# The 64-token block inverse of a chunked recurrence on TensorE: one factor held in the other chunk's half, and products issued by turns

## The chip, the cores and the metric

One core of a Trainium2 chip runs the whole program once. The metric is device microseconds of one execution. A core has TensorE (PE, with its weight loads shown as PEld), VectorE (DVE), ScalarE (ACT), GpSimd (POOL) and the queue engine SyncE (SP), 16 DMA engines, SBUF, and eight PSUM banks.

## The reference

Two transformer blocks of two layers each, 256 tokens, model width 1024, all in fp32. Everything that is changed here belongs to one branch of the second block: a linear recurrence of 8 heads of width 64 with a decaying state, which runs in both layers.

```python
def step(state, inp):
    r_t, w_t, k_t, v_t, a_t, b_t = inp
    sa = jnp.einsum('bhvk,bhk->bhv', state, a_t)
    state = (state * w_t[:, :, None, :] + sa[..., None] * b_t[:, :, None, :]
             + v_t[..., None] * k_t[:, :, None, :])
    return state, jnp.einsum('bhvk,bhk->bhv', state, r_t)
...
y = rwkv7_scan(rh, decay, kh, vh, -kk, kk * ah)
```

Beside it, in the same layer, stand a sparse attention branch (with a top-k search over 256 keys), two sigmoid gates and the output projections; then a memory attention, and a feed-forward or a mixture of experts.

## The kernel before

The 256 tokens are cut into four chunks of 64, and the recurrence inside a chunk is written as matrix products: `AB` holds the products of A with B of all pairs of a chunk's tokens (and those of R with B), `AK` the same with K. The unit lower triangular matrix that belongs to `AB` is inverted block by block: `Tm` and its transpose `TT` start at blocks of 2 and are doubled in five levels, `lv` = 2, 4, 8, 16, 32. A level is X = mask(AB^T Tm) (L1567, then DVE L1570), TT += X^T TT (L1575, DVE L1582) and, but for the last level, Tm += TT^T X (L1580, DVE L1581). With `TT` follow the products by V (L1598), U (L1609), the transform WT of A (L1619), and then the serial part over the four chunks: U += WT S (L1636, DVE L1638), the next state from K, V, B and U (L1642, L1644), and the outputs (L1667, L1674).

All these are products of 64 by 64 matrices. A product that reads partitions 0 to 63 uses the upper half of the array's rows, one that reads 64 to 127 the lower; the partitions of its PSUM output choose the half of the columns. So a product sits in one of four corners of the array. `half(par)` is the half that holds the even or odd chunk of a pair `t`, `half(hf)` that of a head in a pair of heads `i`, `ch(c)` the columns of chunk c. `bank()` hands out PSUM banks; the recurrence has four of the eight.

One pass of `rwkv_group` handles 4 of the 8 heads, so it runs twice a layer and four times in all (called groups here). The two generators of a layer are advanced by turns. Each `yield n` reports n units of work, and `mixer2` calls so many steps of the dense work of the layer (the columns, gates and projections, L645 and L667, of some 12 matmuls a step, and the sparse attention, L1741 to L1796) for them:

```python
for work in self.rwkv(l, vfirst):
    due[0] += self.RATES[len(ready)] * work
    due[1] += self.RATES[2] * work * len(ready)
```

What is left of the dense work then runs behind. A scheduler of the build sets the final order on each engine. Weights are split into two parts of lower precision by ACT L473 and DVE L474; the top-k search is DVE L1751 to L1757.

Of the kernel before, what the change touches and what calls it, by code (L numbers as in the profile page):

```python
# [14 lines left out]
ALU = mybir.AluOpType  # L15
# [346 lines left out]
class Builder:  # L362
# [967 lines left out]
    def rwkv(self, l, vfirst):  # L1330
# [37 lines left out]
        A.copy(sel, self.ident[0:8, 0:8, None].to_broadcast([8, 8, 64]))  # L1368
# [83 lines left out]
    def rwkv_group(self, l, g, GD, tail, R, K, Vv, WA, ld, w2a, rnT, a0h, kah, nkah, ys, bonus):  # L1452
# [42 lines left out]
        V.scalar_tensor_tensor(f(Bt), f(Bt), 0.5, f(E3), op0=ALU.mult, op1=ALU.mult)  # L1495
        AR = self.t([2, 2, 256], "AR")
        V.scalar_tensor_tensor(AR[:, :, 0], kkn, -1.0, E1, op0=ALU.mult, op1=ALU.mult)
        V.tensor_tensor(AR[:, :, 1], R[:, J], E2, op=ALU.mult)
# [31 lines left out]
        def inside(src, nm):  # L1530

            r = {}
            for hf in range(2):
                b = self.bank().rearrange("p (t j k c) -> p t j k c", t=2, j=2, k=2)
                d = r[hf] = self.t([2, 2, 2, 64], nm)
                for t in range(2):
                    for i in range(2):
                        for par in range(2):
                            c = ch(2 * t + par)
                            PE.matmul(b[half(par), t, i], lhsT=src[half(hf), i, c], rhs=AR[half(hf), i, :, c], start=True, stop=True)  # L1540
                fl = lambda z: z.rearrange("p t j k c -> p (t j) (k c)")
                V.tensor_tensor(fl(d), fl(b), self.cc["kmask"][:, None, :].to_broadcast([P, 4, P]), op=ALU.mult)
            return r
# [5 lines left out]
        for hf in range(2):  # L1549
            b = self.bank().rearrange("p (u c) -> p u c", u=8)  # L1550
            for t in range(2):
                for i in range(2):
                    for par in range(2):
                        c = ch(2 * t + par)
                        PE.matmul(b[half(par), 2 * t + i], lhsT=AR[half(hf), i, 0, c], rhs=Bt[half(hf), i, c], start=True, stop=True)
            V.tensor_tensor(Tm[:, hf], b[:, 0:4], m8("lv1", 4), op=ALU.mult)
            V.tensor_tensor(TT[:, hf], AB[hf].rearrange("p t j k c -> p (t j) k c")[:, :, 0], m8("lv1T", 4), op=ALU.mult)
# [5 lines left out]
        for lv in (2, 4, 8, 16, 32):  # L1563
            b = self.bank().rearrange("p (u c) -> p u c", u=8)
            for u, (hf, t, i) in enumerate(un):
                for par in range(2):
                    PE.matmul(b[half(par), u], lhsT=AB[hf][half(par), t, i, 0], rhs=Tm[half(par), hf, 2 * t + i],  # L1567
                              start=True, stop=True)
# [24 lines left out]
        for k in range(2):  # L1593
            b = self.bank().rearrange("p (t c) -> p t c", t=2)
            for t in range(2):
# [4 lines left out]
            if k == 0:  # L1600
                self.evac(akv, b)
            else:
                A.copy(yg, b.rearrange("p t (h c) -> p t h c", h=4))
            yield 1
        b = self.bank().rearrange("p (t c) -> p t c", t=2)
        for t in range(2):
            for h in range(4):
                for par in range(2):
                    PE.matmul(b[half(par), t, hc(h)], lhsT=TT[half(par), h % 2, 2 * t + h // 2], rhs=akv[half(par), t, hc(h)],  # L1609
                              start=True, stop=True)  # L1610
# [3 lines left out]
        WT = self.t([2, 4, 64], "WT")  # L1614
        for par in range(2):
            b = self.bank().rearrange("p (u c) -> p u c", u=8)
            for t in range(2):
                for h in range(4):
                    PE.matmul(b[half(h % 2), 2 * t + h // 2], lhsT=At[half(par), t, hc(h)], rhs=TT[half(par), h % 2, 2 * t + h // 2],  # L1619
                              start=True, stop=True)  # L1620
            self.evac(WT[:, par], b[:, 0:4])
# [8 lines left out]
        for c in range(4):  # L1630
# [39 lines left out]
            for hf in range(2):  # L1670
                b = self.bank().rearrange("p (u c) -> p u c", u=8)
                for cc in range(max(1, 2 * t), 2 * t + 2):
                    for i in range(2):
                        PE.matmul(b[half(cc % 2), i], lhsT=Rt[half(hf), i, ch(cc)], rhs=Sb[cc][half(hf), i], start=True, stop=True)  # L1674
# [612 lines left out]
```

## Time and profile before

| what | value |
|---|---|
| median of 3 runs | 2567.77 us (2567.64 to 2573.2) |
| the profiled execution's own time | 2573.59 us |
| its span | 2571.8 us, 40556 instructions |
| PE busy | 2498.0 us, 97% |
| PEld busy | 2129.9 us, 83% |
| DVE busy | 1936.2 us, 75% |
| ACT busy | 1319.6 us, 51% |
| chain that ended last | PE 88%, DVE 7%, ACT 2%, DMA 2% |

The profile is of one execution. A busy engine is one that has an instruction under way; matmuls overlap, so the busy time of PE says less than how far the starts of its bursts lie apart. Each fp32 matmul of the program appears in the trace as two matmul records, so counts there are twice those of the program's order. PEclk is the granted share of TensorE's clock, 1.00 being 2.4 GHz and 0.50 being 1.2 GHz.

### The profile page before, as it was taken

The numbers are of one execution on the slowest core, as the hardware profiler recorded it, in microseconds if no ns is written. First come the engines' busy times: TensorE is split into PE (matmuls) and PEld (weight loads), VectorE is DVE, ScalarE is ACT, GpSimd is POOL, SyncE is SP. The second block draws the span as 40 slices with busy tenths as digits, with TensorE's granted clock in tenths as the row PEclk, the third lists the DMA queues.
The fourth block names the chain that finished last, engine by engine and source line by source line (L and its number), as shares of the span: only waits on it lengthen the run. The fifth ranks groups of instructions, "written<-read, shape, count | busy, mean of one in ns | idle before, by whom it ended". The sixth has DMA issues, their size and how long they took to land.

```text
span 2571.8 us, 40556 instructions
## 1 busy us (share of the span) xinstructions
PE 2498.0 (97%) x16346; PEld 2129.9 (83%) x16346; DVE 1936.2 (75%) x3247; ACT 1319.6 (51%) x1967; POOL 75.6 (3%) x77
## 2 busy tenths in 40 slices
PE   8999999999999999999999998999999988999998
PEld 7887788888888788888888877888988877888887
DVE  6779767777777676777686478778685577999998
ACT  4445444444444444544544445445434345788786
POOL 0001000000000000000010000000100000000000
PEclk9999999999999999999999989999999998999999
DMA  6445344554564353555413244555211336998995
GB/s 258 180 176 197 130 165 151 193 200 173 184 226 169 142 203 154 184 193 190 177 34 117 97 164 148 184 200 195 104 63 60 140 121 240 355 344 337 346 337 199
DMA packets 77716, 477.74 MB, mean 186 GB/s; under 512 B 9936, under 2 KB 14928, under 8 KB 26832
## 3 DMA queue, kind: packets, MB, share of 16 engines
q1 hardware_dynamic: 77520, 475.06, 50.2%
q8 instruction: 130, 2.13, 0.3%
q14 instruction: 66, 0.54, 0.1%
HBM read 473.98 MB, written 1.05 MB: 185 GB/s over the span
## 4 chain that ended last, share of the span: by engine, by line
PE 88%; DVE 7%; ACT 2%; DMA 2%; issue 1%; SPq 0%; POOL 0%; DVEq 0%; ACTq 0%
PE bank L581 18%; PE bank L903 11%; PE bank L2076 9%; PE bank L582 9%; PE bank L645 8%; PE bank L717 6%; PE bank L2036 5%; PE bank L667 3%; PE bank L685 3%; DVE area L474 3%; PE bank L701 1%; PE bank L741 1%; PE bank L995 1%; DMA area<-w 1%; PE bank L1567 1%
## 5 line engine op out<-in xcount | busy, mean ns | idle before, releaser
L473 ACT ACTIVATE area<-area 128x1024 fp32r<-128x1024 f32 (+4 forms) x981 | 944.5, 975 | 714.8 <-PE bank L581 249.4
L474 DVE TENSOR_TENSOR area<-area,area 128x1024 fp32r<-128x1024 f32 (+4 forms) x981 | 1070.4, 1115 | 263.2 <-ACT area L473 258.5
L581 PE MATMUL bank<-area 128*128 128x512 f32 x2208 | 790.5, 400 | 4.0 <-DVE area L474 3.0
L582 PE MATMUL bank<-area 128*128 128x256 f32 x2208 | 619.1, 282 | 0.4 <-DVE area L474 0.4
L581 PEld LDWEIGHTS bank<-area 128*128 128x128 f32 x2208 | 415.2, 188 | 111.4 <-issue 6.8
L582 PEld LDWEIGHTS bank<-area 128*128 128x128 f32 x2208 | 417.8, 189 | 8.0 <-DVE area L474 2.1
L903 PE MATMUL bank<-area 128*128 128x512 f32 x1320 | 323.5, 396 | 4.0 <-ACT area L473 2.4
L903 PEld LDWEIGHTS bank<-area 128*128 128x128 f32 x1320 | 244.3, 190 | 59.2 <-DVE area L474 4.3
L586 DVE TENSOR_REDUCE area<-bank 128x256 f32<-128x512 f32 x276 | 190.2, 689 | 89.2 <-PE bank L582 88.5
L2076 PE MATMUL bank<-area 128*128 128x512 f32 (+1 forms) x1152 | 257.0, 373 | 0.0
L645 PE MATMUL bank<-area 128*128 128x256 f32 x1824 | 243.8, 290 | 1.4 <-ACT area L473 1.4
L645 PEld LDWEIGHTS bank<-area 128*128 128x128 f32 x1824 | 228.4, 195 | 7.2 <-ACT area L473 2.6
L2076 PEld LDWEIGHTS bank<-area 128*128 128x128 f32 x1152 | 209.6, 188 | 29.9
L717 PE MATMUL bank<-area 128*128 128x512 f32 x672 | 160.6, 395 | 2.4 <-DVE area L748 1.6
L717 PEld LDWEIGHTS bank<-area 128*128 128x128 f32 x672 | 125.1, 189 | 28.7 <-DVE area L748 2.0
L473 ACT ACTIVATE area<-bank 128x512 fp32r<-128x512 f32 (+2 forms) x154 | 82.9, 565 | 93.8 <-PE bank L741 34.5
L2036 PE MATMUL bank<-area 128*128 128x512 f32 x528 | 131.0, 392 | 0.0
L474 DVE TENSOR_TENSOR area<-bank,area 128x512 fp32r<-128x512 f32 (+2 forms) x154 | 97.0, 645 | 39.4 <-ACT area L473 39.3
L749 POOL TENSOR_TENSOR area<-area 128x1 f32<-128x1 f32 (+3 forms) x68 | 68.8, 1012 | 1902.2 <-DVE area L748 1780.6
L2036 PEld LDWEIGHTS bank<-area 128*128 128x128 f32 x528 | 97.6, 188 | 18.9
L950 ACT COPY area<-bank 128x512 f32<-128x512 f32 (+1 forms) x103 | 50.7, 498 | 99.0 <-PE bank L995 39.7
L685 PE MATMUL bank<-area 128*128 128x512 f32 x384 | 96.5, 401 | 3.7 <-ACT area L473 2.0
(281 smaller groups left out, 2231.1 us busy)
## 6 DMA issues: line engine op xcount, KB each, us to landing
area<-w SPq DMA_DIRECT2D x396, 1024.0 KB, 4.9
area<-w SPq DMA_DIRECT2D x32, 768.0 KB, 6.0
area<-rows SPq DMA_DIRECT2D x24, 512.0 KB, 6.7
area<-w SPq DMA_DIRECT2D x10, 512.0 KB, 5.5
area<-mem SPq DMA_DIRECT2D x8, 512.0 KB, 6.5
area<-cbias SPq DMA_DIRECT2D x8, 512.0 KB, 6.1
area<-w SPq DMA_DIRECT2D x2, 800.0 KB, 6.4
area<-x SPq DMA_DIRECT2D x2, 512.0 KB, 5.4
```

The lines of the kernel that those rows point to most:

```text
L473: return (self.A.activation(hi, src, AF.Copy), self.V.tensor_tensor(lo, src, hi.bitcast(F32), op=ALU.subtract))
L474: self.V.tensor_tensor(lo, src, hi.bitcast(F32), op=ALU.subtract))
L581: self.PE.matmul(bank[:, : 2 * n].rearrange("p (u c) -> p u c", u=2), lhsT=a[0], rhs=b.both, start=start, stop=False)
L582: self.PE.matmul(bank[:, n : 2 * n], lhsT=a[1], rhs=b[0], start=False, stop=stop)
L586: return self.V.tensor_reduce(out, ps.rearrange("p (u c) -> p c u", u=2), axis=AX.X, op=ALU.add)
L645: self.PE.matmul(bank[:, g * 256 : g * 256 + 256], lhsT=a, rhs=b, start=j == 0, stop=j == 3 * kt - 1)
L667: self.PE.matmul(bank[:, t, :n], lhsT=a[:, t, k], rhs=b, start=k == 0 and j == 0, stop=k == kt - 1 and j == 2)
L685: self.PE.matmul(bank[:, :n], lhsT=a[:, t, k], rhs=b, start=k == 0 and j == 0, stop=k == kt - 1 and j == 2)
L717: self.PE.matmul(acc[t][h], lhsT=a[:, t, k], rhs=b, start=k == 0 and j == 0, stop=k == kt - 1 and j == 2)
L903: self.PE.matmul(acc[t][h], lhsT=a[:, t * P : (t + 1) * P], rhs=b, start=m == 0 and j == 0, stop=m == n - 1 and j == 2)
L2036: self.PE.matmul(acc[hh], lhsT=x[:, k, :], rhs=y, start=c0 == 0 and k == 0 and j == 0, stop=c0 + n == E_DIM and k == n // P - 1 and j == 2)
L2076: PE.matmul(bk, lhsT=x[:, k, i * P : (i + 1) * P], rhs=y, start=k == 0 and j == 0, stop=k == 7 and j == 2)
```

## The change

`AR`, which holds A and R, is written with the two chunks of a pair exchanged, by four products instead of two, and its sign moves into the selector matrix (-1 in place of 1) and into B. So a matrix that is the left factor of one chunk sits in the half of the other one, and `Tm` and `X` come to lie in another half than `AB` and `TT`. The first `TT` is now made by products of its own (L1562) instead of being taken out of `AB`. In the levels, the two products that end a level are issued by turns, two corners for one (L1584) and two for the other (L1586); `inside` (L1541) goes through both heads of a pair by turns, the products by V (L1605) through both right-hand sides, and those of WT (L1626) through both chunks. Two banks are held at a time where one was before. A level below 32 yields 2 units where it yielded 3, and the products by V 1 where they yielded 2.

```diff
-        V.scalar_tensor_tensor(f(Bt), f(Bt), 0.5, f(E3), op0=ALU.mult, op1=ALU.mult)
+        V.scalar_tensor_tensor(f(Bt), f(Bt), -0.5, f(E3), op0=ALU.mult, op1=ALU.mult)
...
-        V.scalar_tensor_tensor(AR[:, :, 0], kkn, -1.0, E1, op0=ALU.mult, op1=ALU.mult)
-        V.tensor_tensor(AR[:, :, 1], R[:, J], E2, op=ALU.mult)
+        v4 = lambda z, a: z.rearrange("p j (t a c) -> p j t a c", t=2, a=2)[:, :, :, a]
+        for a in range(2):
+            V.tensor_tensor(v4(AR[:, :, 0], 1 - a), v4(kkn, a), v4(E1, a), op=ALU.mult)
+            V.tensor_tensor(v4(AR[:, :, 1], 1 - a), v4(R[:, J], a), v4(E2, a), op=ALU.mult)
...
-            for hf in range(2):
-                b = self.bank().rearrange("p (t j k c) -> p t j k c", t=2, j=2, k=2)
-                d = r[hf] = self.t([2, 2, 2, 64], nm)
-                for t in range(2):
-                    for i in range(2):
+            r, b = {}, [self.bank().rearrange("p (t j k c) -> p t j k c", t=2, j=2, k=2) for _ in range(2)]
+            for t in range(2):
+                for i in range(2):
+                    for hf in range(2):
                         for par in range(2):
                             c = ch(2 * t + par)
-                            PE.matmul(b[half(par), t, i], lhsT=src[half(hf), i, c], rhs=AR[half(hf), i, :, c], start=True, stop=True)
+                            PE.matmul(b[hf][half(par), t, i], lhsT=src[half(hf), i, c], rhs=AR[half(hf), i, :, ch(2 * t + 1 - par)], start=True, stop=True)
...
+                for hf in range(2):
+                    for par in range(2):
+                        c = ch(2 * t + par)
+                        PE.matmul(b[hf][half(1 - par), 1, 2 * t + i], lhsT=Bt[half(hf), i, c], rhs=AR[half(hf), i, 0, ch(2 * t + 1 - par)], start=True, stop=True)
...
-            V.tensor_tensor(TT[:, hf], AB[hf].rearrange("p t j k c -> p (t j) k c")[:, :, 0], m8("lv1T", 4), op=ALU.mult)
+            V.tensor_tensor(TT[:, hf], b[hf][:, 1], m8("lv1T", 4), op=ALU.mult)
...
-                    PE.matmul(b[half(par), u], lhsT=AB[hf][half(par), t, i, 0], rhs=Tm[half(par), hf, 2 * t + i],
+                    PE.matmul(b[half(1 - par), u], lhsT=AB[hf][half(par), t, i, 0], rhs=Tm[half(par), hf, 2 * t + i],
...
-            b2 = self.bank().rearrange("p (u c) -> p u c", u=8)
+            b1, b2 = [self.bank().rearrange("p (u c) -> p u c", u=8) if z else None for z in (lv < 32, True)]
             for u, (hf, t, i) in enumerate(un):
-                for par in range(2):
-                    PE.matmul(b2[half(par), u], lhsT=X[half(par), u], rhs=TT[half(par), hf, 2 * t + i], start=True, stop=True)
+                v = 2 * t + i
+                for q in range(2):
+                    PE.matmul(b2[half(q), u], lhsT=X[half(q), u], rhs=TT[half(q), hf, v], start=True, stop=True)
+                for q in range(2 if lv < 32 else 0):
+                    PE.matmul(b1[half(1 - q), u], lhsT=TT[half(q), hf, v], rhs=X[half(q), u], start=True, stop=True)
             if lv < 32:
-                b1 = self.bank().rearrange("p (u c) -> p u c", u=8)
-                for u, (hf, t, i) in enumerate(un):
-                    for par in range(2):
-                        PE.matmul(b1[half(par), u], lhsT=TT[half(par), hf, 2 * t + i], rhs=X[half(par), u], start=True, stop=True)
                 V.tensor_tensor(fu(Tm), fu(Tm), b1, op=ALU.add)
             V.tensor_tensor(fu(TT), fu(TT), b2, op=ALU.add)
-            yield 1 + (lv < 32)
+            yield 1
...
-        for k in range(2):
-            b = self.bank().rearrange("p (t c) -> p t c", t=2)
-            for t in range(2):
-                for h in range(4):
+        bs = [self.bank().rearrange("p (t c) -> p t c", t=2) for _ in range(2)]
+        for t in range(2):
+            for h in range(4):
+                for k in range(2):
                     for par in range(2):
-                        PE.matmul(b[half(par), t, hc(h)], lhsT=AK[h % 2][half(par), t, h // 2, k], rhs=vt[half(par), t, hc(h)],
-                                  start=True, stop=True)
+                        PE.matmul(bs[k][half(par if k else 1 - par), t, hc(h)], lhsT=AK[h % 2][half(par), t, h // 2, k],
+                                  rhs=vt[half(par), t, hc(h)], start=True, stop=True)
...
+        bs = [self.bank().rearrange("p (u c) -> p u c", u=8) for _ in range(2)]
+        for t in range(2):
+            for j in range(2):
+                for par in range(2):
+                    for x in range(2):
+                        h = 2 * j + x
+                        PE.matmul(bs[par][half(x), 2 * t + j], lhsT=At[half(1 - par), t, hc(h)], rhs=TT[half(1 - par), x, 2 * t + j],
+                                  start=True, stop=True)
```

The end of one level on PE in the first layer, before. Each row is a run of matmuls of one line into one bank; L1483 belongs to the other group, L645 is dense work:

```order
L1483 MATMUL bank_68<-area_63 128x256 x2
L1036 MATMUL bank_72<-area_63 128x128 x2
L1575 MATMUL bank_67<-area_63 64x64 x16
L1580 MATMUL bank_65<-area_63 64x64 x16
L645 MATMUL bank_71<-area_64 128x256 x9
```

The same place in the change (the pair of lines goes on by turns up to x16 each):

```order
L1483 MATMUL bank_68<-area_63 128x256 x2
L645 MATMUL bank_71<-area_64 128x256 x4
L1584 MATMUL bank_65<-area_63 64x64 x2
L1586 MATMUL bank_67<-area_63 64x64 x2
L1584 MATMUL bank_65<-area_63 64x64 x2
L1586 MATMUL bank_67<-area_63 64x64 x2
```

The two products of a level, 16 matmuls behind 16 before, now change places after every two, between two banks.

The end of the serial tail on PE in the first layer, before: states, outputs and the output's gate and transposes (L1442, L1447), up to the branch's projection (L645):

```order
L1442 MATMUL bank_68<-area_63 128x256
L1667 MATMUL bank_65<-area_63 64x64
L1636 MATMUL bank_66<-area_63 64x64 x2
L1636 MATMUL bank_67<-area_63 64x64 x2
L1667 MATMUL bank_65<-area_63 64x64 x2
L1674 MATMUL bank_66<-area_63 64x64 x4
L1667 MATMUL bank_65<-area_63 64x64 x5
L1674 MATMUL bank_67<-area_63 64x64 x4
L1442 MATMUL bank_65<-area_63 128x256
L1447 MATMUL bank_68<-area_63 128x128 x2
```

The same place in the change, where L1675, L1644 and L1682 are the former L1667, L1636 and L1674:

```order
L1442 MATMUL bank_67<-area_63 128x256
L645 MATMUL bank_72<-area_64 128x256 x10
L1675 MATMUL bank_65<-area_63 64x64
L1644 MATMUL bank_68<-area_63 64x64 x2
L1644 MATMUL bank_66<-area_63 64x64 x2
L1675 MATMUL bank_65<-area_63 64x64 x2
L1682 MATMUL bank_68<-area_63 64x64 x4
L1447 MATMUL bank_67<-area_63 128x128 x2
L1675 MATMUL bank_65<-area_63 64x64 x5
L1682 MATMUL bank_66<-area_63 64x64 x4
```

Dense work now stands in this stretch. Behind the first state product of the tail the program has 180 matmuls of L645 before the branch's projection in either layer, and with the change 290 in the first layer and 288 in the second.

## Rows read from the trace of the kernel before

**Rows 1.** The page, the chain that ended last, by engine.

```profile
PE 88%; DVE 7%; ACT 2%; DMA 2%; issue 1%; SPq 0%; POOL 0%; DVEq 0%; ACTq 0%
```

**Rows 2.** Windows, both layers: us, busy PE, PEld, DVE, ACT, POOL; PEclk, DMA, GB/s.

```profile
1301.00:1338.00 37.00, 37.00 (x444) 32.98 (x442) 32.95 (x73) 14.00 (x28) 3.50 (x3) 1.00 0.09 30
1338.00:1362.00 24.00, 23.09 (x331) 19.81 (x330) 22.81 (x96) 8.19 (x20) 0.56 (x1) 1.00 0.24 84
1362.00:1451.00 89.00, 89.00 (x1255) 78.77 (x1256) 43.57 (x89) 38.22 (x77) 3.84 (x4) 1.00 0.19 66
1451.00:1508.00 57.00, 50.70 (x524) 44.47 (x522) 37.46 (x112) 21.69 (x38) 4.93 (x4) 0.85 0.43 158
...
1884.00:1915.00 31.00, 26.73 (x376) 24.04 (x376) 28.72 (x98) 7.41 (x17) 0.56 (x1) 0.86 0.01 2
1915.00:2010.00 95.00, 95.00 (x1335) 83.85 (x1332) 48.45 (x109) 40.52 (x85) 3.84 (x4) 0.99 0.24 85
2010.00:2065.00 55.00, 49.28 (x527) 43.02 (x526) 37.51 (x113) 21.05 (x38) 4.03 (x4) 0.91 0.45 159
```

**Rows 3.** Windows around the stretches at half clock in the two tails.

```profile
1466.00:1470.00 4.00, 4.00 (x43) 3.35 (x44) 3.81 (x10) 3.50 (x4) 1.85 (x1) 0.57 0.78 322
1493.00:1508.00 15.00, 12.92 (x92) 10.36 (x92) 8.29 (x40) 3.55 (x10) 2.06 (x2) 0.54 0.01 2
2049.00:2061.00 12.00, 10.41 (x99) 8.22 (x100) 8.35 (x41) 2.20 (x6) 1.74 (x2) 0.57 0.01 1
```

**Rows 4.** Groups by line: line, engine, operation, shape, count, busy us, mean ns.

```profile
L1575 PE MATMUL bank<-area 64*64 64x64 f32 x640 | 25.5, 222 | 0.0
L1580 PE MATMUL bank<-area 64*64 64x64 f32 x512 | 20.8, 220 | 0.0
L1598 PE MATMUL bank<-area 64*64 64x64 f32 x256 | 9.9, 221 | 0.0
L1555 PE MATMUL bank<-area 64*64 64x64 f32 x128 | 5.3, 224 | 0.0
```

**Rows 5.** Timeline of PE, one level's end: start, us from first start to last end, group.

```profile
1319.46 1.15 PE L1575 MATMUL bank<-area 64*64 64x64 f32 x32
1320.44 1.10 PE L1580 MATMUL bank<-area 64*64 64x64 f32 x32
```

**Rows 6.** Timeline of PE where bursts on two row halves meet.

```profile
1303.65 0.28 PE L1540 MATMUL bank<-area 64*64 64x128 f32 x2
1303.66 0.28 PE L1555 MATMUL bank<-area 64*64 64x64 f32 x4
1303.76 0.28 PE L1540 MATMUL bank<-area 64*64 64x128 f32 x2
```

**Rows 7.** Timeline of PE, bursts between dense work, 1417 to 1457 us.

```profile
1417.90 1.59 PE L1540 MATMUL bank<-area 64*64 64x128 f32 x32
1419.42 1.69 PE L667 MATMUL bank<-area 128*128 128x256 f32 x12
...
1423.75 1.15 PE L1598 MATMUL bank<-area 64*64 64x64 f32 x32
1424.83 1.70 PE L667 MATMUL bank<-area 128*128 128x256 f32 x12
1426.45 1.15 PE L1575 MATMUL bank<-area 64*64 64x64 f32 x32
...
1455.99 0.98 PE L1619 MATMUL bank<-area 64*64 64x64 f32 x32
```

**Rows 8.** The chain that ended last: dense work behind dense work.

```profile
1370.83 1.44 PE bank L667 x12
```

**Rows 9.** DVE groups of the widths that the change uses.

```profile
L1498 DVE TENSOR_TENSOR area<-area 128x512 f32<-128x512 f32 x4 | 2.8, 688 | 1.5 <-ACT area L1466 1.5
L1438 DVE TENSOR_TENSOR area<-area 128x256 f32<-128x256 f32 x8 | 3.4, 422 | 4.5 <-ACT area L1437 4.5
L1556 DVE TENSOR_TENSOR area<-bank,area 128x256 f32<-128x256 f32 x8 | 3.3, 415 | 0.1
```

More of the change, by code (lines that the diff above doesn't have):

```diff
@@ L1367, in rwkv @@
         sel = self.t([8, 64], "sel64")[0:8]
-        A.copy(sel, self.ident[0:8, 0:8, None].to_broadcast([8, 8, 64]))
+        A.activation(sel, self.ident[0:8, 0:8, None].to_broadcast([8, 8, 64]), AF.Copy, scale=-1.0)
         self.sel = sel.rearrange("p h d -> p (h d)")
@@ L1548, in rwkv_group @@
         m8 = lambda n, k: self.cc[n][:, None, :].to_broadcast([P, k, 64])
-        for hf in range(2):
-            b = self.bank().rearrange("p (u c) -> p u c", u=8)
-            for t in range(2):
-                for i in range(2):
+        b = [self.bank().rearrange("p (x u c) -> p x u c", x=2, u=4) for _ in range(2)]
+        for t in range(2):
+            for i in range(2):
+                for hf in range(2):
                     for par in range(2):
                         c = ch(2 * t + par)
-                        PE.matmul(b[half(par), 2 * t + i], lhsT=AR[half(hf), i, 0, c], rhs=Bt[half(hf), i, c], start=True, stop=True)
-            V.tensor_tensor(Tm[:, hf], b[:, 0:4], m8("lv1", 4), op=ALU.mult)
-            V.tensor_tensor(TT[:, hf], AB[hf].rearrange("p t j k c -> p (t j) k c")[:, :, 0], m8("lv1T", 4), op=ALU.mult)
+                        PE.matmul(b[hf][half(par), 0, 2 * t + i], lhsT=AR[half(hf), i, 0, ch(2 * t + 1 - par)], rhs=Bt[half(hf), i, c], start=True, stop=True)
+                for hf in range(2):
+                    for par in range(2):
+                        c = ch(2 * t + par)
+                        PE.matmul(b[hf][half(1 - par), 1, 2 * t + i], lhsT=Bt[half(hf), i, c], rhs=AR[half(hf), i, 0, ch(2 * t + 1 - par)], start=True, stop=True)
+        for hf in range(2):
+            V.tensor_tensor(Tm[:, hf], b[hf][:, 0], m8("lv1", 4), op=ALU.mult)
+            V.tensor_tensor(TT[:, hf], b[hf][:, 1], m8("lv1T", 4), op=ALU.mult)
         fu = lambda z: z.rearrange("p a u c -> p (a u) c")
@@ L1592, in rwkv_group @@
         akv, U = self.t([2, 256], "akv"), self.t([2, 256], "U")
-        for k in range(2):
-            b = self.bank().rearrange("p (t c) -> p t c", t=2)
-            for t in range(2):
-                for h in range(4):
+        bs = [self.bank().rearrange("p (t c) -> p t c", t=2) for _ in range(2)]
+        for t in range(2):
+            for h in range(4):
+                for k in range(2):
                     for par in range(2):
-                        PE.matmul(b[half(par), t, hc(h)], lhsT=AK[h % 2][half(par), t, h // 2, k], rhs=vt[half(par), t, hc(h)],
-                                  start=True, stop=True)
[L1600 to L1604, printed above, removed]
+                        PE.matmul(bs[k][half(par if k else 1 - par), t, hc(h)], lhsT=AK[h % 2][half(par), t, h // 2, k],
+                                  rhs=vt[half(par), t, hc(h)], start=True, stop=True)
+        self.evac(akv, bs[0])
+        A.copy(yg, bs[1].rearrange("p t (h c) -> p t h c", h=4))
+        yield 1
         b = self.bank().rearrange("p (t c) -> p t c", t=2)
@@ L1608, in rwkv_group @@
                 for par in range(2):
-                    PE.matmul(b[half(par), t, hc(h)], lhsT=TT[half(par), h % 2, 2 * t + h // 2], rhs=akv[half(par), t, hc(h)],
+                    PE.matmul(b[half(par), t, hc(h)], lhsT=TT[half(1 - par), h % 2, 2 * t + h // 2], rhs=akv[half(1 - par), t, hc(h)],
                               start=True, stop=True)
@@ L1614, in rwkv_group @@
         WT = self.t([2, 4, 64], "WT")
-        for par in range(2):
[L1616 to L1621, printed above, removed]
+        bs = [self.bank().rearrange("p (u c) -> p u c", u=8) for _ in range(2)]
+        for t in range(2):
+            for j in range(2):
[4 more added lines that the diff above has]
+                                  start=True, stop=True)
+        for par in range(2):
+            self.evac(WT[:, par], bs[par][:, 0:4])
         Rt = self.t([2, 256], "Rt")
@@ L1673, in rwkv_group @@
                     for i in range(2):
-                        PE.matmul(b[half(cc % 2), i], lhsT=Rt[half(hf), i, ch(cc)], rhs=Sb[cc][half(hf), i], start=True, stop=True)
+                        PE.matmul(b[half(cc % 2), i], lhsT=Rt[half(hf), i, ch(cc ^ 1)], rhs=Sb[cc][half(hf), i], start=True, stop=True)
                 p0 = 0 if t else 64
```

4 lines of the change are left out of this document (2 added, 2 removed).

## Prediction

> **What bounds the kernel now.** I read the page's chain first: TensorE carries 88% of it [rows 1], so the change can pay on TensorE, but only where TensorE is the engine that the others wait for. The windows by stage say where that is [rows 2]. The recurrence runs in two stretches, one per layer of the second block: 1301 to 1508 us and 1854 to 2065 us. In 1362 to 1451 and 1915 to 2010 PE is busy to the last digit (89.00 of 89.00 us, 95.00 of 95.00) while DVE is half idle: what TensorE no longer has to do there shortens the time. In 1301 to 1338 PE is as full, with DVE at 32.95 of 37.00 close behind. In 1338 to 1362 and 1884 to 1915 DVE is busy 22.81 of 24.00 and 28.72 of 31.00 us (the top-k search of the sparse attention), and PE is idle 0.9 and 4.3 us: what TensorE saves ahead of these ends may turn into waiting. In the two tails, 1451 to 1508 and 2010 to 2065, PE is idle 6.3 and 5.7 us and the granted clock averages 0.85 and 0.91: the serial chunk steps run there, at half clock (0.54 and 0.57) in the last part [rows 3].
>
> Each fp32 matmul stands in the trace as two records, which I call passes (the plan's x16 is the trace's x32).
>
> **The products of the block inverse.** For the levels 2 to 16, L1575 and L1580 run 32 passes each, back to back; in 4 groups (2 layers by 2) and 4 levels that is 1024 of their 1152 passes (640 and 512) [rows 4]. A block of 32 takes 1320.44 - 1319.46 = 0.98 us, so 30 ns a pass, although one pass lasts 222 ns: passes already overlap, in pairs, because the two chunks sit in two corners of the array (rows and columns 0 to 63, rows and columns 64 to 127) [rows 4, 5]. Both lines use the same two corners, so the other two stand empty. The change puts L1586 in the other two and issues the lines by turns.
>
> Whether four corners run at once is visible today, where two bursts on different row halves meet. At 1303.65 two wide passes (L1540, upper rows) and four narrow ones (L1555, lower rows) start in each 0.11 us [rows 6]; alone, the two wide ones would take 2 x 1.52 / 32 us = 0.095 us [rows 7] and the four narrow ones 4 x 30 = 0.12 us, 0.215 together. So the row halves hardly disturb each other: 6 passes in 110 ns is 18 ns a pass. Likewise L1619 (one row half, then the other) takes 0.98 us as one burst where L1598 takes 1.15 [rows 7]. I take 18 ns; the ends are 15 ns (two rows' worth at once with no loss) and 30 ns (no gain).
>
> - Levels: 1024 x (30 - 18) ns = 12.3 us (ends 15.4 and 0).
> - L1598 [rows 4]: two bursts of 32 per group become one of 64 over four corners: 256 x 12 ns = 3.1 us (3.8 and 0). One excursion into the small shapes costs (1424.83 - 1423.75) - 32 x 30 ns = 0.12 us, and the L667 x12 behind it takes 1426.45 - 1424.83 = 1.62 us where the same 12 behind dense work take 1.44, so 0.3 us in all [rows 7, 8]; 4 are saved: 1.2 us.
> - L1619, one such burst a group: 128 x 12 ns = 1.5, less the 4 x 0.17 us that the meeting of its halves already gives: 0.8 us (0.5 to 1.2).
> - L1540: 8 bursts, two a group, of 1.52 us become 8 rounds of four passes, 0.11 us each, plus 0.15 to enter: 1.0. Saved 8 x 0.5 = 4.0 us (0 to 5).
> - L1555: the change adds as many passes again, 128 [rows 4]; 128 x 30 ns before, 256 x 18 after: +0.8 us (0 to +3.8).
>
> Together 20.6 us; with nothing overlapped a loss of 2.6, with everything 25.6.
>
> **DVE.** The two 512-wide operations that write AR (688 ns for the second; the first is as wide) become four of 256 at 422 ns: 4 x 422 - 2 x 688 = 0.3 us a group, 1.3 in all, hidden by PE except near the DVE-bound windows [rows 9]. I charge 1.0. The mask product that now reads PSUM costs nothing: L1556, with a PSUM source of that size, takes 415 ns, L1438 from SBUF 422 [rows 9]. The sign on the selector is one ACT instruction for another, once a layer: nothing.
>
> **Work lost at the DVE-bound windows.** Of each layer's 8 level blocks some 3, and 2 of its 4 L1540 pairs, lie ahead of the end of these windows: 3 x 0.77 + 2 x 0.5 = 3.3 us a layer. I take half as lost: 3.3 us of 6.6.
>
> **The filler that moves.** Each group now yields 5 units of work fewer, so 10 a layer, and the dense filler (12 matmuls to a step) is called by these units. In the plan 290 instead of 180 of the filler's matmuls stand behind the first step of the serial tail in the first layer, 288 instead of 180 in the second. At 1.44 / 12 = 0.12 us each [rows 8], 110 make 13.2 us a layer that move from the PE-bound part into the tail. Where PE is busy throughout, that is neither gain nor loss. In the tail it can fill idle time (12.0 us over both layers) and hold the clock (the half-clock windows hold 12.9 and 10.4 us of PE work, nearly half of it lost, 12 us with the small dip at 1466) [rows 2, 3]. At most 24 us come back, at least none; a filler block also stands ahead of the next recurrence step in TensorE's order, so I take a third: 8 us.
>
> **Sum.** 20.6 - 1.0 - 3.3 + 8.0 = 24.3 us. The profiled execution took 2573.59 us, 5.8 us above the median of the three runs (2567.77), so it would be 2549; from the median I forecast 2543 us. About 0.3%, 8 us, is what a measurement of this kernel can tell from no change.
>
> **The rule that speaks against it.** The rows show 18 ns a pass where four corners work [rows 6]. The Trainium skill ("TensorE: Matmul & The Clock Gate", Part 1, "Wait — 56ns, not 53.3ns?") says that matmuls do not start closer than some 25 ns apart, however small they are. By that rule 30 ns could only fall to 25, and the forecast would be the rival A below. The trace disagrees as far as its 0.3 us go; that a queue filled beforehand fed them is not excluded.
>
> The same skill ("TensorEngine Tiling (Array Packing)", Gotcha 1) says that different row tiles cannot use one PSUM bank at the same time. L1575 contradicts it here: its two chunks are two row tiles that write the halves of one bank, and overlap at 30 ns a pass against 222 for one [rows 4, 5]. If it held for the new mix, rival C would follow.
>
> **Rivals.**
> - A, a start limit. Sustained over 64 passes, TensorE starts one per 25 ns and no faster. Levels and L1598 give 1280 x 5 ns = 6.4, L1540 still 4.0 (27 ns a pass already), the merged bursts 1.2, L1555 loses 256 x 25 - 128 x 30 = 2.6: 9.0. With 8.0 from the tail, less 1.0 and half the DVE loss, 14.4: 2553 us. For it: no stretch of four corners lasts longer than 0.3 us today.
> - B, DVE swallows it. All 6.6 us are lost and the tail gives nothing: 20.6 - 1.3 - 6.6 = 12.7, 2555 us. For it: DVE in 1338 to 1362. Against: it is half idle in the long windows.
> - C, the change does not do what it says: the four corners do not run together. -2.6 + 8 - 1 = +4.4 us, 2563 us. Rows 6 speak against.
> - D, the tail gives all 24 instead of 8: 2527 us.
> - E, slower. The 13.2 us of filler a layer queue ahead of the chunk steps in TensorE's order and lengthen the tail by their full time, while the stretch ahead does not get shorter, since DVE and ACT pace it and PE waits: 26.4 + 1.3 - 12.0 (tail idle filled) = 15.7, 2583 us. It decides once PE idles by more than some 10 us a layer ahead of the tail; today it idles 0.9 and 4.3 us there [rows 2].
>
> **Chances and range.** The forecast 0.50 (its own range 2533 to 2552), D 0.13, A 0.13, B 0.11, C 0.07, E 0.06. The range from 2522 (all of the overlap or all of the tail) to 2561 (below C) leaves out less than 2 in 10. Faster by over 0.3% (below 2560): nearly all of the forecast, D and A, most of B, 0.82; within it C and the rest, 0.11; slower 0.07.
>
> **What would show it.** Right: the level lines alternate with some 1.1 us for 64 passes instead of 2.0; PE idle in the tails below 4 us and fewer half-clock windows; the stretches 207 and 211 us long now each 10 to 15 us shorter. Wrong: 64 passes still near 1.6 us (A) or 2.0 (C); PE idle of more than 5 us ahead of each tail (B, E); tails much longer than 57 and 55 us with idle time kept (E).

## The result, and the profile after

| what | before | change |
|---|---|---|
| median | 2570.48 us (2567.64 to 2575.17, 4 runs) | 2544.22 us (2543.18 to 2547.95, 4 runs) |
| ratio | | 0.9896 [0.9881, 0.9912] |
| the profiled execution | 2573.59 us | 2547.95 us |

The change saves 1.04%, some 26 to 27 us. The forecast was 2543 us from a median of 2567.77 (a gain of 24.8). A second measurement of the change, on another chip, gave 0.9894 [0.9879, 0.9909]. The page of the change, its span, its engines and its chain (its last line is to be read beside [rows 1]):

```profile
span 2546.1 us, 40839 instructions
...
PE 2473.4 (97%) x16474; PEld 2107.6 (83%) x16474; DVE 1935.6 (76%) x3255; ACT 1320.1 (52%) x1967; POOL 77.7 (3%) x77
...
PE 87%; DVE 7%; DMA 2%; ACT 1%; issue 1%; SPq 0%; POOL 0%; DVEq 0%; ACTq 0%; POOLq 0%
```

Neither the busy shares nor the chain shows the gain; the stages do. I cut each layer's recurrence at two marks that both kernels have: from its first L1540 (L1541 now) to the first product of the serial steps, "ahead of the tail", and from there to the first product of the next part (L717), "the tail". Windows of the kernel before, cut so: us, busy PE, PEld, DVE, ACT, POOL; PEclk, DMA, GB/s.

```profile
1301.20:1451.30 150.10, 149.19 (x2026) 131.67 (x2025) 99.13 (x256) 60.40 (x125) 7.90 (x8) 1.00 0.17 60
1451.30:1516.80 65.50, 59.06 (x593) 52.94 (x593) 43.70 (x121) 25.49 (x42) 4.93 (x4) 0.87 0.41 149
1858.60:2010.70 152.10, 147.83 (x2000) 131.50 (x1998) 97.60 (x247) 58.39 (x123) 7.21 (x8) 0.96 0.15 55
2010.70:2074.10 63.40, 57.26 (x594) 51.08 (x593) 43.76 (x122) 25.13 (x42) 4.03 (x4) 0.92 0.42 148
```

The same of the change (they answer to [rows 2]):

```profile
1306.50:1439.90 133.40, 128.62 (x1981) 111.98 (x1980) 94.55 (x254) 54.13 (x118) 9.14 (x8) 0.97 0.16 55
1439.90:1513.00 73.10, 68.89 (x701) 63.45 (x701) 49.08 (x126) 30.95 (x49) 4.03 (x4) 0.95 0.43 157
1850.70:1980.00 129.30, 124.66 (x1958) 108.97 (x1957) 90.04 (x244) 53.11 (x115) 8.94 (x8) 0.97 0.13 46
1980.00:2052.60 72.60, 67.66 (x702) 62.61 (x702) 48.38 (x127) 30.60 (x49) 4.03 (x4) 0.98 0.45 164
```

Over both layers the part ahead of the tails went from 302.2 to 262.7 us, the tails from 128.9 to 145.7. Together that is -22.7 us, of 25.7 between the spans (2571.8, 2546.1); what is left lies outside the changed code, where two profiles of the change itself differ by as much (the first L1541 stands at 1306.5 us in one and at 1302.5 in the other). PE's idle time, window less busy, rose from 5.2 to 9.4 us ahead of the tails and fell from 12.6 to 9.1 in them, and the clock of the tails rose from 0.87 and 0.92 to 0.95 and 0.98.

How the levels run now, on PE's timeline (start, us from first start to last end, group; left out are 28 rows of the same pattern):

```profile
1325.48 0.27 PE L1584 MATMUL bank<-area 64*64 64x64 f32 x2
1325.49 0.27 PE L1586 MATMUL bank<-area 64*64 64x64 f32 x2
1325.58 0.23 PE L1584 MATMUL bank<-area 64*64 64x64 f32 x2
1325.60 0.23 PE L1586 MATMUL bank<-area 64*64 64x64 f32 x2
...
1326.57 1.10 PE L645 MATMUL bank<-area 128*128 128x256 f32 x7
```

Four passes, one in each corner, start every 58 ns, and the block of 64 takes 1326.57 - 1325.48 = 1.09 us, from its first start to the dense work behind it. In the kernel before, that dense work stood at

```profile
1321.47 0.39 PE L645 MATMUL bank<-area 128*128 128x256 f32 x1
```

so the same block took 1321.47 - 1319.46 = 2.01 us [rows 5]. Ten of the sixteen blocks run whole like this one; the others are split among other work. A pass itself is no shorter than before [rows 4], so all of it is overlap:

```profile
L1584 PE MATMUL bank<-area 64*64 64x64 f32 x640 | 26.8, 223 | 3.8 <-DVE area L1578 3.8
L1586 PE MATMUL bank<-area 64*64 64x64 f32 x512 | 22.6, 224 | 0.0
L1605 PE MATMUL bank<-area 64*64 64x64 f32 x256 | 7.8, 225 | 0.0
L1558 PE MATMUL bank<-area 64*64 64x64 f32 x128 | 7.6, 223 | 0.0
```

The first row also shows the price: PE now waits 3.8 us for X (DVE L1578), where the line stood at 0.0 before. The waits of PE ahead of the first tail, then of the second (us in total, times, longest):

```profile
PE bank L1787 <- DVE area L474: 2.3, 1, 2.3
PE bank L1584 <- DVE area L1578: 1.0, 1, 1.0
PE bank L1575 <- DVE area L1588: 0.7, 1, 0.7
PE bank L1787 <- ACT area L1752: 0.5, 1, 0.5
PE bank L1787 <- ACT area L1815: 0.2, 1, 0.2
...
PE bank L1584 <- DVE area L1578: 2.8, 1, 2.8
PE bank L1787 <- DVE area L474: 1.8, 1, 1.8
```

All but 0.7 us are on DVE. In the second layer DVE is in rounds of the top-k search then (L1764, L1765); in the first it is partly in other work of the sparse attention and in the splits (L474).

Not every group is issued as it is written. In the built order some bursts stand bank by bank, so that mostly two corners work at a time. Two L1541 bursts of 32 in one layer, the first bank by bank, the second by turns:

```profile
1407.88 1.58 PE L1541 MATMUL bank<-area 64*64 64x128 f32 x32
1409.39 0.62 PE L667 MATMUL bank<-area 128*128 128x256 f32 x3
...
1426.72 1.10 PE L1541 MATMUL bank<-area 64*64 64x128 f32 x32
1427.75 0.62 PE L667 MATMUL bank<-area 128*128 128x256 f32 x3
```

1.51 us for one and 1.03 for the other, beside 1.52 before [rows 7]. In half of the four groups L1558 and L1562 also stand bank by bank: four passes each 0.115 us (1313.49, 1313.61, 1313.73), 30 ns a pass:

```profile
1313.49 0.28 PE L1558 MATMUL bank<-area 64*64 64x64 f32 x4
1313.61 0.28 PE L1562 MATMUL bank<-area 64*64 64x64 f32 x4
1313.73 0.28 PE L1558 MATMUL bank<-area 64*64 64x64 f32 x4
```

### The profile page after: what moved, and what is told of

The parts are those of the page before. It is cut to its first block, busy times and chain, and to the rows that moved or that the text cites. A ratio compares the mean times of both kernels' runs of the same rounds, so it can differ in the third digit from the quotient of the medians.

```text
span 2546.1 us, 40839 instructions
## 1 busy us (share of the span) xinstructions
PE 2473.4 (97%) x16474; PEld 2107.6 (83%) x16474; DVE 1935.6 (76%) x3255; ACT 1320.1 (52%) x1967; POOL 77.7 (3%) x77
## 4 chain that ended last, share of the span: by engine, by line
PE 87%; DVE 7%; DMA 2%; ACT 1%; issue 1%; SPq 0%; POOL 0%; DVEq 0%; ACTq 0%; POOLq 0%
PE bank L581 19%; PE bank L903 11%; PE bank L2084 9%; PE bank L582 9%; PE bank L645 8%; PE bank L717 5%; PE bank L2044 5%; PE bank L667 3%; DVE area L474 3%; PE bank L685 3%; DMA area<-w 2%; PE bank L701 1%; PE bank L995 1%; PE bank L741 1%; PE bank L1575 1%
## 5 line engine op out<-in xcount | busy, mean ns | idle before, releaser
L473 ACT ACTIVATE area<-area 128x1024 fp32r<-128x1024 f32 (+4 forms) x981 | 945.5, 975 | 741.7 <-PE bank L581 250.3
L474 DVE TENSOR_TENSOR area<-area,area 128x1024 fp32r<-128x1024 f32 (+4 forms) x981 | 1072.0, 1117 | 268.0 <-ACT area L473 263.7
L645 PE MATMUL bank<-area 128*128 128x256 f32 x1824 | 248.9, 293 | 1.9 <-ACT area L473 1.2
L645 PEld LDWEIGHTS bank<-area 128*128 128x128 f32 x1824 | 231.3, 196 | 8.6 <-ACT area L473 1.9
L717 PE MATMUL bank<-area 128*128 128x512 f32 x672 | 159.8, 394 | 2.4 <-DVE area L748 1.3
L717 PEld LDWEIGHTS bank<-area 128*128 128x128 f32 x672 | 124.6, 188 | 28.3 <-DVE area L748 1.8
L474 DVE TENSOR_TENSOR area<-bank,area 128x512 fp32r<-128x512 f32 (+2 forms) x154 | 97.3, 649 | 43.4 <-ACT area L473 43.3
L473 ACT ACTIVATE area<-bank 128x512 fp32r<-128x512 f32 (+2 forms) x154 | 82.7, 564 | 84.0 <-PE bank L741 31.2
L758 ACT ACTIVATE area<-area 128x1024 f32<-128x1024 f32 x32 | 35.4, 1106 | 123.2 <-DVE area L850 83.9
```

The source lines that it names most:

```text
L473: return (self.A.activation(hi, src, AF.Copy), self.V.tensor_tensor(lo, src, hi.bitcast(F32), op=ALU.subtract))
L474: self.V.tensor_tensor(lo, src, hi.bitcast(F32), op=ALU.subtract))
L645: self.PE.matmul(bank[:, g * 256 : g * 256 + 256], lhsT=a, rhs=b, start=j == 0, stop=j == 3 * kt - 1)
L717: self.PE.matmul(acc[t][h], lhsT=a[:, t, k], rhs=b, start=k == 0 and j == 0, stop=k == kt - 1 and j == 2)
```

## The experiments

All are compared with the kernel before on the same chip. The trace columns come from one profile each, cut at the same marks, both layers added up: the part ahead of the tails, PE's idle time in it, the tails.

| run | median us | ratio to before | ahead | PE idle | tails |
|---|---|---|---|---|---|
| before | | | 302.2 | 5.2 | 128.9 |
| change | 2544.22 | 0.9896 [0.9881, 0.9912] | 262.7 | 9.4 | 145.7 |
| change again | 2546.33 | 0.9894 [0.9879, 0.9909] | 262.5 | 9.6 | 145.8 |
| e1 units of work only | 2566.20 | 0.9977 [0.9965, 0.9988] | 284.5 | 11.1 | 146.0 |
| e2 corners only | 2552.15 | 0.9924 [0.9910, 0.9939] | 283.0 | 6.2 | 131.5 |
| e3 level in a row | 2545.89 | 0.9901 [0.9884, 0.9919] | 268.2 | 6.1 | 146.1 |
| e4 turns, same corners | 2571.21 | 0.9996 [0.9984, 1.0008] | 303.8 | 5.1 | 128.4 |
| e5 corners, in a row | 2556.09 | 0.9932 [0.9919, 0.9946] | 285.7 | 1.0 | 131.1 |
| e6 change, short search | 2534.26 | 0.9847 [0.9827, 0.9867] | 249.2 | 2.2 | 148.5 |
| e7 in a row, short search | 2548.82 | 0.9908 [0.9893, 0.9923] | 259.2 | 1.6 | 146.0 |
| e8 other turns undone | 2550.05 | 0.9915 [0.9897, 0.9933] | 265.8 | 8.7 | 147.2 |
| e9 before, short search | 2561.32 | 0.9966 [0.9952, 0.9980] | 296.5 | 1.8 | 129.9 |
| b1 filler early | 2544.74 | 0.9903 [0.9886, 0.9921] | 268.5 | 9.2 | 140.6 |
| b2 search in pieces | 2545.74 | 0.9906 [0.9888, 0.9923] | 259.3 | 8.1 | 142.8 |

### The two halves of the change, and corners against turns

**e1**, the kernel before with the change's units of work, so only the filler moves:

```diff
-            yield 1 + (lv < 32)
+            yield 1
...
-            yield 1
+        yield 1
```

> The kernel before, with only the units of work of the change (a level below 32 yields 2 in all, the products by V 1), so that 108 of the dense matmuls move into each tail and no product changes its corner. Theory 1 (the corners pay most, the moved filler some): 8 us less than before, about 2562 us, PE idle in the tails falling from 12.6 us by a third. Theory 2 (the moved filler pays most): 14 us less or better, 2556 us or below. Theory 3 (the moved filler costs): 2571 us or above.

Measured: 0.9977, -5.9 us (-9.0 to -3.1). The tails with the filler in them:

```profile
1450.00:1523.30 73.30, 70.61 (x702) 64.73 (x702) 49.03 (x125) 30.81 (x49) 4.03 (x4) 0.95 0.44 158
...
2003.20:2075.90 72.70, 67.79 (x701) 62.80 (x702) 48.56 (x127) 31.01 (x50) 4.03 (x4) 0.98 0.44 163
```

PE's idle time there falls from 12.6 to 7.6 us and the clock is that of the change. The tails grow by 17.1 us where 216 matmuls of 0.12 us, 25.9 us, came in: 8.8 come back. (A dense matmul stands once in the trace, unlike the 64 by 64 ones: x593 became x702.) Ahead of the tails the stretch shrinks by 17.7 instead of 25.9: idle time doubles there (11.1), and in the first layer the granted clock is 0.94 where it was 1.00. In the profile the two stretches and tails together are thus only 0.6 us shorter. It was the slowest of twelve executions (2571.06 us), so the loss may stand too high in it; the gain of 5.9 us rests on the times alone.

**e2**, the other half: the change with the units of before.

```diff
-            yield 1
+            yield 1 + (lv < 32)
...
-        yield 1
+        yield 2
```

> The changed kernel with the units of work of the kernel before, so that the filler in the tails is 180 matmuls a layer again. Theory 1: it keeps two thirds of the gain, about 2552 us; the tails look as before (PE idle 6 us each). Theory 2: it keeps less than half, 2557 us or above. Theory 3: faster than the change, below 2544 us.

Measured: 0.9924, -19.5 us. 0.9977 x 0.9924 = 0.9901, beside 0.9896 and 0.9894 of the whole: the halves add up. The tails are much like those of before (131.5 us beside 128.9, clock 0.87 in both).

**e3**, the four corners stay, but the two products of a level stand one behind the other:

```diff
                 for q in range(2):
                     PE.matmul(b2[half(q), u], lhsT=X[half(q), u], rhs=TT[half(q), hf, v], start=True, stop=True)
+            for u, (hf, t, i) in enumerate(un):
+                v = 2 * t + i
                 for q in range(2 if lv < 32 else 0):
```

> The changed kernel with the two products of a level one behind the other again, in four corners but not by turns. If the queue needs the turns to fill the four corners: 64 passes take about 1.9 us instead of 0.95, with some overlap at the meeting point, so 16 blocks cost 12 to 15 us of PE and the time rises by 8 to 14 us to 2552 to 2558 us. If TensorE looks far enough ahead by itself: 64 passes stay near 1.0 us and the time at 2544 us.

PE's timeline of one level (L1588 is the second product in this kernel; seven rows of the meeting are left out):

```profile
1320.00 0.97 PE L1584 MATMUL bank<-area 64*64 64x64 f32 x26
1320.76 0.27 PE L1588 MATMUL bank<-area 64*64 64x64 f32 x2
...
1320.93 0.98 PE L1588 MATMUL bank<-area 64*64 64x64 f32 x27
1321.84 0.86 PE L645 MATMUL bank<-area 128*128 128x256 f32 x5
```

The block takes 1.84 us instead of 1.09: though the corners are free, the second product starts only at the end of the first, and the two overlap for 0.17 us. Turns are needed for the overlap. The passes of the two lines take 37.7 us ahead of the tails against 25.3 (counted as in the table of terms below), and PE's busy time there is 262.2 us against 253.3. Yet the ratio is only 0.0005 to 0.0007 above the change's (about 1.5 us, give or take 5), and the stretch 5.5 us longer. So something else takes part of it.

**e4**, the kernel before with the two products by turns in its two old corners:

```diff
             for u, (hf, t, i) in enumerate(un):
                 for par in range(2):
                     PE.matmul(b2[half(par), u], lhsT=X[half(par), u], rhs=TT[half(par), hf, 2 * t + i], start=True, stop=True)
+                for par in range(2 if lv < 32 else 0):
+                    PE.matmul(b1[half(par), u], lhsT=TT[half(par), hf, 2 * t + i], rhs=X[half(par), u], start=True, stop=True)
```

> The kernel before with the two products of a level by turns, but in the same two corners. If the corners are what pays: 64 passes stay at 1.9 us and the time at 2570 us within 4 us. If the turns pay by themselves: 64 passes near 1.0 us, and 8 to 14 us less.

Measured: 0.9996, nothing, and its whole blocks take 2.01 us as before. With e3: for the overlap of the two products, other corners and turns are both needed.

### Who takes what the turns save

**e5**, e2 and e3 together (units of before, corners of the change, levels in a row).

> The changed kernel with the units of work of the kernel before (as in the run with the corners only) and the two products of a level one behind the other. Theory 1 (the turns save TensorE some 0.75 us for each of 16 blocks, and in the changed kernel the wait for DVE behind the top-k search swallows most of it, because the filler that covered it went into the tail): here, with the filler in place, the turns show, so this is 6 to 12 us slower than the run with the corners only, 2558 to 2564 us. Theory 2 (the turns are worth nothing anywhere): 2552 us within 3 us.

Measured: 2556.09 us, below what theory 1 named, and only 0.0008 above e2 (some 2 us, give or take 5), as theory 2 has it. So it is not the moved filler that swallows the turns. The stretches tell more: between e5 and e2 PE's busy time falls from 284.7 to 276.8, and its idle time rises from 1.0 to 6.2. The second layer of e5, then of e2:

```profile
1857.40:1998.90 141.50, 141.36 (x2064) 125.03 (x2063) 95.81 (x250) 58.67 (x122) 7.39 (x8) 1.00 0.16 55
...
1844.40:1988.00 143.60, 139.24 (x2064) 122.65 (x2062) 97.60 (x249) 58.99 (x123) 7.08 (x8) 0.95 0.15 54
```

There, in one profile of each, the stretch is 2.1 us longer with the turns: PE has less to do, but waits 4.4 us instead of 0.1, and its granted clock is 0.95 instead of 1.00. Most of the wait is one, for what follows the search's masks; the kernel before has the like (L741 for DVE L1786, 4.3 us):

```profile
PE bank L741 <- DVE area L1794: 3.7, 1, 3.7
```

This run also says what the level's turns are not. With neither them nor the moved filler e5 keeps 0.9932, 17.5 us of the change's 26 to 27. Of the 12.4 us by which PE's busy time ahead of the tails falls from before to e5 (297.0 to 284.7), 4.6 lie on L1541 and 3.6 on the products by V, both by turns over four corners, and 2.0 on the lines of the levels; PE's idle time is 4.1 us lower beside.

**e6**, the change with one round of the top-k search in place of eight (it leaves out the other seven), and **e7**, the same with the levels in a row as in e3:

```diff
-            for r in range(8):
+            for r in range(1):
```

> The changed kernel with one round of the top-k search in place of eight, so fewer keys are masked out and DVE has some 2 x 14 x 0.7 = 20 us less to do in both layers. Theory 1 (PE waits for DVE there): the 4.8 and 4.6 us of PE idle ahead of the tails shrink below 2 us each and the time falls by 5 to 10 us, to 2534 to 2539 us. Theory 2 (DVE is covered): 2544 us within 3 us.

> The same with the two products of a level one behind the other. Theory 1: with DVE out of the way the turns show: 6 to 12 us slower than the changed kernel with the short search, against 2 us with the full one. Theory 2 (the turns are worth nothing anywhere): the same within 3 us.

Windows ahead of the tails, e6:

```profile
1302.00:1429.30 127.30, 125.13 (x1981) 109.54 (x1980) 85.60 (x212) 54.43 (x118) 9.15 (x8) 0.99 0.17 57
...
1842.30:1964.20 121.90, 121.84 (x1957) 107.10 (x1956) 82.22 (x202) 53.38 (x115) 8.82 (x8) 0.97 0.15 48
```

And e7:

```profile
1299.10:1431.70 132.60, 131.26 (x1983) 115.73 (x1982) 86.05 (x212) 54.38 (x118) 9.14 (x8) 0.99 0.16 55
...
1848.60:1975.20 126.60, 126.31 (x1958) 111.11 (x1960) 82.51 (x202) 53.18 (x116) 8.79 (x8) 1.00 0.14 47
```

With DVE relieved, PE's waits shrink to 2.2 and 0.1 us. All the waits for DVE that are left in e6:

```profile
PE bank L1584 <- DVE area L1578: 1.9, 1, 1.9
PE bank L1575 <- DVE area L1588: 0.3, 1, 0.3
```

What the level's turns are worth, in three surroundings:

| surroundings | the levels' two lines | PE busy saved | PE idle added | stretch shorter | by the times |
|---|---|---|---|---|---|
| units of before (e5, e2) | 12.7 | 7.9 | 5.2 | 2.7 | some 2 +- 5 |
| change (e3, change) | 12.4 | 8.9 | 3.4 | 5.5 | some 1.5 +- 5 |
| short search (e7, e6) | 11.6 | 10.6 | 0.6 | 10.0 | 15.7 +- 6.4 |

The saving on the two lines is much the same in each. With the full search 5.2 and 3.4 us of it turn into waiting, mostly for DVE, and another 4.8 and 3.5 are lost on PE's other lines; that these run more at half clock (in the trace's clock record 13.7 us of e2's stretches against none of e5's, 13.7 of the change's against 10.2 of e3's) is part of it, the rest stays open. With the short search next to nothing turns into waiting. The times agree in direction. They show 15.7 where the stretches show 10.0, and 7.5 with the tails, which are 2.5 us longer in e6; the other way, e7's profile loses 5.1 us at half clock (10.2 us) between the two layers, outside the changed code.

**e8**, the change with the other turns undone (only the loop order of L1541, L1605 and L1626; of each the moved loop is shown):

```diff
-            for t in range(2):
-                for i in range(2):
-                    for hf in range(2):
+            for hf in range(2):
+                for t in range(2):
+                    for i in range(2):
...
-        for t in range(2):
-            for h in range(4):
-                for k in range(2):
+        for k in range(2):
+            for t in range(2):
+                for h in range(4):
...
-        for t in range(2):
-            for j in range(2):
-                for par in range(2):
+        for par in range(2):
+            for t in range(2):
+                for j in range(2):
```

> The change with the turns of the three other product groups undone: L1541 again one row half behind the other, L1605 one k behind the other, L1626 one chunk half behind the other; corners, merged bursts, levels by turns and units of work stay. My sum gave these turns 3.1 + 0.8 + 4.0 = 7.9 us of TensorE's work. If TensorE's work counted in full wherever it is saved (the prediction's sum), +6 to +9 us against the changed kernel. If the search on DVE takes what is saved ahead of the tails (theory 2, as in the level's case, where some 12 us of TensorE's work were worth 1 to 2 us of time), only L1605, L1626 and the part of L1541 in the stretches where DVE has room count: 0 to +4 us.

Measured: 2550.05 us, 0.0019 to 0.0021 above the change (5 us, give or take 5); by the stretches 3.1 ahead of the tails and 1.5 in them. The times lie between the two expectations and decide nothing; the trace says 4.6, so these turns pay most of what they save on PE (3.8 ahead of the tails).

**e9**, the kernel before with the short search of e6.

> The kernel before with one round of the top-k search instead of eight (it leaves out seven of the eight rounds). Theory 2 (DVE's search is what swallows the turns): the stretches ahead of the tails are short of TensorE alone in the kernel before, so the short search brings this kernel at most 2 to 6 us (PE idle 0.9 and 4.3 us ahead of the tails), 2566 to 2570 us, and the change with the short search gains 32 to 36 us against it (its own time was 2534), more than with the full search (26). The rival, that the short search saves the same in both kernels: 2558 to 2562 us, a gain of 26.

Measured: 2561.32 us, -8.7 us (-12.3 to -5.1), inside what the rival named: the kernel before loses time to the search too. The change's gain with the short search is 0.9847 / 0.9966 = 0.9881, 30.5 us give or take 6, beside 27 with the full one: the times can't tell the two apart. By the stretches and tails it is 426.4 - 397.7 = 28.7 us beside 22.7. So the search costs the change some 6 us more than it cost the kernel before, in one profile of each; the rival's "same in both" is not excluded by the times, and theory 2's 2566 to 2570 us for this run was missed.

### Two tries to get it back

**b1** puts filler back, but behind the first two levels, where DVE is late:

```diff
-            yield 1
+            yield 1 + (lv < 8)
```

> The changed kernel with a second unit of work (so a second block of filler) behind the levels 2 and 4 of each group, none behind 8 and 16: of the filler 36 matmuls a layer go back from the tail into the stretch ahead of it. Theory 2: PE idles there 4 to 5 us and could take them for nothing while the tail gets 36 x 0.12 = 4.3 us a layer shorter, less what the tail then idles (it would idle up to 1.5 us more): 2 to 6 us below the changed kernel. Rival (the waits fall at places where no filler is at hand, and the order decides): within 2 us of it, or a loss as in the run with the units of before, +6.

Measured: no gain. 5.1 us left the tails and 5.8 came in ahead of them; PE idles there as much as before (9.2 us), but at other places. Its longest waits, in the first layer and in the second:

```profile
PE bank L667 <- ACT area L473: 4.8, 1, 4.8
...
PE bank L1575 <- DVE area L1588: 3.0, 1, 3.0
```

Half of the idle time is now dense work that waits for its own split on ACT (L473). So the rival's time came out, though the waits moved rather than stayed; whether the place of this filler brought that about is not shown.

**b2** hands out the search in pieces of two rounds:

```diff
                 V.match_replace(score[:, :nk], m8, score[:, :nk], -3.0e38)
+                if r % 2 == 1 and r < 7:
+                    yield
...
-    RATES = (1.4, 0.85, 0.35)
+    RATES = (1.4, 0.85, 0.5)
```

> The changed kernel with the top-k search handed out in pieces of two rounds (so that DVE's work on the levels can come between them) and the third part's share of work per unit raised from 0.35 to 0.5. Theory 2: the waits of TensorE for DVE ahead of the tails (4 to 5 us of PE idle, and half clock) shrink, as far as the search can be spread: 2 to 8 us below the changed kernel, at most the 10 to 12 us that the short search gave. Rival: the sum of DVE's work in this stretch is the limit, not its lumps: within 2 us.

Measured: 2545.74 us (2537.78 to 2548.05), no gain in the median. Its profiled execution was the fastest of its four, so the 6.3 us that its stretches and tails show are no evidence. Neither try beats the change.

## Why the prediction was right, point by point

The total was right to 2 us of the gain, in part by luck: terms that came out larger and smaller cancel (below), and 3.0 us of the gain between the two profiles lie outside the changed code. The two ends given for the sum of the terms, -2.6 and 25.6, come to -2.1 and 26.6 from the terms as they stand, and 2522 us needs all of the overlap and all of the tail; the forecast does not hang on either. Its terms, each in the two stretches and tails (one profile): on PE a line's time is what lies between the start of each of its passes and the start of the next pass of any line, idle time left out.

| term | predicted | found |
|---|---|---|
| levels (L1575, L1580) | -12.3 | -14.9 (40.2 to 25.3) |
| X's product (L1567) | 0 | -2.0 (27.4 to 25.4) |
| L1598 by turns, bursts merged | -4.3 | -2.5 (8.8 to 6.3) |
| L1540 | -4.0 | -2.3 (13.8 to 11.5) |
| L1619 (half of it lies ahead of the tails) | -0.8 | -0.6 (1.5 to 0.9) |
| L1555 doubled | +0.8 | +3.3 (4.5 to 7.8) |
| all other lines, beyond the filler that left (216 x 0.12 us) | 0 | +1.2 |
| PE's work together | -20.6 | -17.8 |
| lost to DVE | +4.3 | +4.2 (idle 5.2 to 9.4) |
| regained in the tails | -8.0 | -9.1 (25.9 in, 16.8 longer) |
| sum | -24.3 | -22.7 |

- **Levels: the mechanism was right; the term was too small for PE's work and too large for the time.** I took 18 ns a pass with ends of 15 and 30; rounds of four start every 58 ns, 15 ns a pass, and with the entry a block is 1.09 / 64 us = 17 ns. At 2.01 - 1.09 = 0.92 us each, sixteen whole blocks would give 14.7. What the terms do not say is what this is worth: with the turns taken out again (e3), the two lines lose 12.4 us, but the stretches and tails only 5.9 and the times 1.5, give or take 5. Of the 12.3 us that the sum put on the levels about half is to be seen there.
- **Rival A is refuted.** It wanted 25 ns between starts over 64 passes, 1.6 us. The rule behind it, of the Trainium skill ("TensorE: Matmul & The Clock Gate", Part 1, "Wait — 56ns, not 53.3ns?"), that matmuls do not start closer than some 25 ns, does not hold here: 64 passes start in about a microsecond, in four corners. It was neither a short queue nor a short stretch that made the 18 ns of [rows 6].
- **Rival C is refuted** by the same rows, as four corners do run together. The rule of the Trainium skill ("TensorEngine Tiling (Array Packing)", Gotcha 1) that row tiles cannot use one PSUM bank at once does not keep this mix apart: L1584's two passes come from the two row halves and write the two halves of one bank, in each 58 ns round, and each lasts 223 ns. At which moment of a pass its bank is written, the trace does not show.
- **L1540, L1598 and L1555: the step that failed** is that I gave each the price of four corners, 18 ns a pass, as if issued in the order written. The built order has several bursts bank by bank (L1541 1.51 us beside 1.03; L1558 and L1562 30 ns a pass) and L1605 cut into pieces (2, 12, 8 and 10 passes in each layer before a whole burst of 32). The three terms fall short by 1.7, 1.8 and 2.5 us, 6.0 together; the levels give 2.6 of it back, and X's product 2.0, which had no term and whose cause is not shown. The order in which the changed kernel's instructions stand shows the cuts without any run.
- **DVE: right in size, by two guesses together.** I charged 3.3 us as half of what is saved ahead of the search's end, and 1.0 for the wider AR writes. PE's idle time rose by 4.2, in waits for L1578 and L474. The experiments show who: with the short search 2.2 us of idle time are left of 9.4, and the stretches are 10.0 instead of 5.5 us shorter by the level's turns. Rival B, that DVE takes all of it and the tail gives nothing, was half true of the level's turns and wrong of the tails.
- **The tail: the mechanism was right, the size a guess.** PE's idle time in the tails fell from 12.6 to 9.1 us and the clock rose; 9.1 us came back of 24 at most. The third that was taken is worked out from no row. Alone (e1) this half brought 5.9 us. Rival E's turning point, some 10 us of idle time a layer ahead of the tails, stayed far (4.8 and 4.6 us). D, all 24 us, was far as well.
- **What should have shown it:** the 1.1 us for 64 passes are there (1.09). Idle time below 4 us in each tail is not (4.2 and 4.9), though the half-clock stretches of the tails are shorter (27.3 to 10.2 us in the trace's clock record). The two stretches, tails included, are 9.1 and 13.6 us shorter where 10 to 15 were named, so the first just misses.

## What to carry to other kernels

Small products that leave part of the array empty are worth spreading over it, but two things are needed at once: operands that lie in the other half, and an order by turns. A level's block took 1.84 us with the corners alone (e3), 2.01 with the turns alone (e4) and 1.09 with both. Read the built order for each group before pricing it, since a scheduler may take the turns apart again. And price a saving on one engine at the stage: of some 12 us that the level's turns save on their own lines, 3 to 6 reached the stretches beside the full search and 10 beside the short one.

## What was not expected of the hardware

- Four 64 by 64 corners ran wholly independently: a round of four starts every 58 ns, as a round of two did before (2 x 30 ns). The two added corners cost nothing.
- TensorE did not reach far ahead of its order, but a little: in e3, where all of L1584 stands ahead of L1588 in the built order, the first L1588 starts at 1320.76 us and the last L1584 at 1320.93, 0.17 us behind it.
- Where PE does the same work, its clock makes 3.4 us of difference between two profiles of one kernel, in a stretch that the change doesn't touch (between the layers 337.7 us with nothing at half clock, 341.1 with 6.8 us of it, in the change's two profiles). Differences of 5 us between two kernels need the stretches as well as the times.
